# A decoder layer's early products: one of them in four chains, one copy out of the banks, and another order for VectorE

## The chip, the cores and the metric

The kernel runs on one core of a Trainium2 chip. The metric is the device time of one execution in microseconds, of which the profile's span (973.2 us before) is the part between the first and the last instruction. TensorE (PE in the rows) multiplies, ScalarE (ACT) and VectorE (DVE) do elementwise work, GpSimd (POOL) a little of it, SyncE (SP) asks for most transfers.

## The reference

One layer, sequence 1024, width 1024, batch 1, all float32:

```python
h = rms_norm(x, pre_g)
z = jnp.einsum('bsd,de->bse', h, w_in)
qa, ka, va, ga, qb, kb, vb, gb, gk_low = split_columns(z)
...
oa = diff_attention(qa, ka, va, lam)
ob = gla_chunked(qb, kb, vb, log_a)
y = jnp.einsum('bse,ed->bsd', jnp.concatenate([oa, ob], axis=-1), w_out)
return x + rms_norm(y, post_g)
```

The change is in the first 100 us, in the first part of `h @ w_in`: the normalised x times the columns vb of the gated values (1024 of them, 512 at a time here) and the first columns of ka.

## The kernel before

**Products.** `h @ w_in` is done with seven products of half-size blocks in place of eight. h is cut in four blocks of 512 x 512 (h11, h12, h21, h22; kept transposed, 4 tiles of 128 rows each, index j), and a group of weight columns likewise (b11, b12, b21, b22). The products are numbered: 1 is h11 b11, 2 is h12 b21, 5 is s1 (b12 - b11), 6 is s2 (b22 - b12 + b11), 7 is s3 (b22 - b12), 4 is h22 (b21 less the sixth's weights), 3 is s4 b22, with s1 = h21 + h22, s2 = s1 - h11, s3 = h11 - h21, s4 = h12 - s2 (in the code with some signs turned). Results go to PSUM banks named x (1, 6, 7), y (2, 4) and z (5, 3). Groups (0,) and (1,) are the gated values, each with two units of 128 rows of the result, so there are four x banks in all; group 2 is a pair of heads of ka with 128 columns to a block.

**Two parts.** Each operand is split in a rounded high part and the rest (h_hi and h_lo, w for both; the type is fp32r), and each product is hi x hi + lo x hi + hi x lo: three matmuls for each of four tiles, 12 of 128x128 by 128x512 to a chain, 48 for both gated groups. The high part is a cast on ScalarE, the low part a subtraction on VectorE.

**Stages.** `load_x` and `load_gated` ask for x and the weights (xs 0 to 3 are named x, 4 to 7 xt; weights are g_raw, `w_early` is for group 2). `norm_x` scales x, the last four tiles on GpSimd. `first(0)` transposes the first half of x's columns for rows 0 to 511 into four banks with spins between (matmuls on zeros whose result is not used) and `put` makes h11's two parts from each bank: the high one by ScalarE, the low one by VectorE, both reading the bank. `first(1)` does the same for h12 and also copies the banks to f1 on ScalarE. `blocks(j)` transposes a tile of h21 and h22 into two banks, which ScalarE copies to t21 and t22 (named t), and makes a tile of s1; `differences(j)` makes s2, s4 and s3's source. `go(n)` does the next n steps of the table `order`, a step being one product of one group; `prepare` makes the weights up to three steps ahead. The sequence at the end of the function is: `first(0)`, a step, `first(1)`, a step, `blocks(0)`, and so on.

**Order.** The engines run their instructions in the order that the framework's scheduler gives. Matmuls and transposes are kept in program order, and so is what is issued while `pinned` is set; the rest is placed by the scheduler, with `tc.issue_after(a)` placing an instruction behind a. L66 is the helper through which all ScalarE, VectorE and GpSimd work is recorded, L142 the helper for matmuls, L145 for transposes, so tiles and not lines tell the groups apart. Banks are taken from the front of the list `free` and put at its end when their last reader has been issued; weights' parts rotate through five buffers (`ring`).

## Time and profile before

| what | us |
| --- | --- |
| median of three runs (976.01 to 976.57) | 976.54 |
| the profiled execution | 974.95 |
| its span | 973.2 |
| TensorE busy in the span | 956.9 |
| TensorE, first matmul of product 1 | 13.95 |
| TensorE, last of product 4 of the gated groups ends | 100.03 |

The times in the rows count from the start of the span. A timeline row gives start, length, engine, line, operation, output and inputs, shapes and the number of instructions merged in it; in brackets the idle time before it and what ended that. A length is that of the instruction; the next one of the same kind may start a little before its end. In a row of waits stand the waiting instruction, the releaser, the sum, the number and the longest.

### The profile page before, as it was taken

The page shows a single profiled execution, that of the slowest core. Times are in us where ns is not written, and L with a number is a line of the kernel's source. Part 1 is how long each engine was busy: PE and PEld are TensorE (multiplying, and loading weights), DVE is VectorE, ACT ScalarE, POOL GpSimd, SP SyncE. Part 2 cuts the span into 40 slices and gives each one's busy share as a digit, 9 for nine tenths or more (in the row PEclk, how much of TensorE's full clock was granted, in tenths as well). Part 3 has the DMA queues.
Part 4 walks back from the last instruction along what each step waited for, and adds up shares of the span by engine and source line. Part 5 has one row for each costly group of instructions (what it writes and reads, how often), then busy time and mean ns, then how long its engine had stood idle before and what let it go on. Part 6 is the DMA issues. An engine that isn't in the chain of part 4 may idle for free.

```text
span 973.2 us, 14406 instructions
## 1 busy us (share of the span) xinstructions
PE 956.9 (98%) x4641; PEld 797.3 (82%) x4641; DVE 736.5 (76%) x1468; ACT 604.8 (62%) x1166; POOL 190.9 (20%) x262
## 2 busy tenths in 40 slices
PE   8889999999999999999999999999999999999997
PEld 6778788888888888888888888878888888888786
DVE  4797699897687686686766576587888888898555
ACT  8653264764667565576765344366776687887773
POOL 3000002222111211231100002121322222443322
PEclk9999999999999999999999999999999999999999
DMA  9424357578667987996864588997656669994777
GB/s 340 157 69 141 95 158 251 184 251 286 210 211 244 291 264 266 286 289 215 253 185 146 169 243 263 402 296 245 221 176 216 240 193 364 335 288 102 152 205 153
DMA packets 152827, 220.36 MB, mean 226 GB/s; under 512 B 15728, under 2 KB 85360, under 8 KB 152656
## 3 DMA queue, kind: packets, MB, share of 16 engines
q1 hardware_dynamic: 138592, 178.70, 57.3%
q0 software_dynamic: 14160, 40.74, 14.2%
q8 instruction: 37, 0.61, 0.3%
q14 instruction: 38, 0.31, 0.1%
HBM read 133.93 MB, written 88.60 MB: 229 GB/s over the span
## 4 chain that ended last, share of the span: by engine, by line
PE 91%; DMA 4%; DVE 2%; SPq 1%; issue 1%; ACT 1%; DVEq 0%; ACTq 0%
PE x L142 23%; PE y L142 15%; PE z L142 14%; PE ypart L142 12%; PE sc L142 6%; PE po L142 5%; PE yps L142 4%; PE wtr L145 3%; PE gpo L142 3%; DMA ks<-k_d 1%; PE kv L142 1%; DMA g_raw<-in_w_in_dram 1%; DMA q_d<-qk_st 1%; PE gkl_ps L142 1%; PE pa L142 1%
## 5 line engine op out<-in xcount | busy, mean ns | idle before, releaser
L66 ACT CAST w<-w_raw 128x512 fp32r<-128x512 f32 x138 | 85.2, 621 | 80.2 <-PE y L142 34.7
L66 ACT ACTIVATE p<-p,stt 128x896 f32<-128x896 f32 (+7 forms) x128 | 99.3, 776 | 36.8 <-DVE stt L66 35.7
L66 DVE TENSOR_TENSOR w<-w_raw,w 128x512 fp32r<-128x512 f32 x138 | 94.3, 687 | 36.6 <-ACT w L66 36.3
L66 ACT COPY s<-x 128x512 f32<-128x512 f32 x78 | 45.2, 586 | 74.8 <-PE x L142 74.5
L66 DVE CUSTOM_DVE_ANT_0 p<-sc,maskt 128x512 f32<-128x512 f32 (+3 forms) x128 | 74.4, 585 | 15.7 <-PE sc L142 14.5
L66 POOL TENSOR_SCALAR p<-p,stt,lam 128x1024 f32<-128x1024 f32 (+3 forms) x64 | 55.9, 873 | 147.9 <-DVE stt L66 144.0
L142 PE MATMUL z<-s_hi,w 128*128 128x512 f32 x320 | 80.2, 393 | 0.0
L142 PE MATMUL x<-s_hi,w 128*128 128x512 f32 x320 | 80.1, 392 | 0.0
L142 PE MATMUL y<-h_hi,w 128*128 128x512 f32 x320 | 80.1, 392 | 0.0
L142 PE MATMUL ypart<-wo_hi,m_hi 128*128 128x512 f32 x192 | 79.5, 414 | 0.1
L142 PE MATMUL ypart<-wo_hi,m_lo 128*128 128x512 f32 x192 | 75.5, 393 | 0.0
L142 PE MATMUL ypart<-wo_lo,m_hi 128*128 128x512 f32 x192 | 75.4, 393 | 0.0
L66 POOL DMA_DIRECT2D wo_d<-wo_hi x32 | 17.4, 544 | 276.3 <-ACT wo_hi L66 276.3
L142 PE MATMUL sc<-k,q 128*128 128x512 f32 (+1 forms) x192 | 69.0, 363 | 1.3 <-DVE stt L66 1.1
L142 PEld LDWEIGHTS z<-s_hi,w 128*128 128x128 f32 x320 | 59.8, 188 | 12.4
L142 PEld LDWEIGHTS x<-s_hi,w 128*128 128x128 f32 x320 | 59.7, 188 | 12.4
L142 PEld LDWEIGHTS y<-h_hi,w 128*128 128x128 f32 x320 | 59.7, 188 | 12.3
L142 PE MATMUL sc<-ks,q 128*128 128x512 f32 (+1 forms) x192 | 66.1, 348 | 0.3 <-DMA ks<-k_d 0.3
L66 ACT CAST wt_hi<-wtr 128x512 fp32r<-128x512 f32 (+1 forms) x80 | 42.8, 535 | 25.3 <-PE wtr L145 24.5
L66 DVE TENSOR_TENSOR w_raw<-w_raw 128x512 f32<-128x512 f32 x80 | 55.3, 691 | 2.8 <-DMA w_raw<-in_w_in_dram 1.9
L66 DVE TENSOR_TENSOR wt_lo<-wtr,wt_hi 128x512 fp32r<-128x512 f32 (+1 forms) x80 | 50.6, 633 | 8.6 <-ACT wt_hi L66 8.0
L66 DVE TENSOR_TENSOR c<-z,s 128x512 f32<-128x512 f32 x48 | 32.9, 689 | 31.1 <-ACT s L66 19.9
(228 smaller groups left out, 2350.8 us busy)
## 6 DMA issues: line engine op xcount, KB each, us to landing
w_raw<-in_w_in_dram SPq DMA_DIRECT2D x40, 512.0 KB, 4.7
wo_d<-wo_hi POOLq DMA_DIRECT2D x32, 256.0 KB, 3.3
q<-q_d SPq DMA_DIRECT2D x32, 256.0 KB, 4.5
k<-k_d SPq DMA_DIRECT2D x32, 256.0 KB, 5.0
ks<-k_d SPq DMA_DIRECT2D x64, 128.0 KB, 5.7
v<-v_d SPq DMA_DIRECT2D x16, 512.0 KB, 7.0
wo_raw<-in_w_out_dram POOLq DMA_DIRECT2D x31, 256.0 KB, 4.7
wo_d<-gqd POOLq DMA_DIRECT2D x22, 256.0 KB, 4.3
```

The lines of the kernel that those rows point to most:

```text
L66: ins = op(*a, **k)
L142: tc.keep_in_program_order(pe.matmul(*a, **k))
L145: tc.keep_in_program_order(pe.transpose(dst, src, ident))
```

## The change

Three things are changed, all ahead of the third column group.

First, product 1 of the gated values. `gated_first` takes the x banks of all four units at once and runs their chains side by side: sixteen matmuls with both high parts, sixteen with h's low part, sixteen with the weights' low part. Between the second and the third part stand `first(1)`'s transposes. The weights' second half is cast after the first two h_hi. One spin fewer stands before it. On TensorE, around the end of the first transposes, before (spin, then x of the first group's two units, then `first(1)`'s transposes xT):

```order
L142 MATMUL spin<-idle,ones 128x512 x4
L142 MATMUL x<-w,h_hi 128x512 x4
L142 MATMUL x<-w,h_lo 128x512 x4
L142 MATMUL x<-w,h_hi 128x512 x8
L145 MATMUL xT<-ident,x_187 128x128 x8
L145 MATMUL xT<-ident,x_190 128x128 x8
```

and now:

```order
L142 MATMUL spin<-idle,ones 128x512 x3
L142 MATMUL x<-w,h_hi 128x512 x16
L142 MATMUL x<-w,h_lo 128x512 x16
L145 MATMUL xT<-ident,x_187 128x128 x2
L145 MATMUL xT<-ident,x_190 128x128 x2
L145 MATMUL xT<-ident,xt 128x128 x8
```

The four chains have become one run of 16, 16 and 16, with the transposes of x between the second and the third, and those of xt behind. (Rows that only repeat are left out: the other chains before, the other banks' transposes and the last sixteen x<-w,h_hi now.)

Second, `first(1)`: ScalarE copies each bank to f1, and h12's two parts are made from f1, not from the bank. Its transposes go bank by bank. The low halves of product 2's weights lie in the buffers that h22's low part takes later, not in the ring.

Third, VectorE's order. s4 and s2 share a buffer and s4 is made after s3; h22's low part is placed behind the sixth product's weights, s3's behind h22's, and the b22 - b12 + b11 subtractions are issued by themselves. `hold` bounds how far weights are prepared. On VectorE, up to the last of the four subtractions that make s2 (s_684<-t_415,t_414 before, the one s_643<-t_440,t_439 in the second listing; f is f1, t are t21 and t22, s_lo are low parts, c and qk_hi belong to group 2, h_lo is h22's low part, the 128x1024 rows are weights), before:

```order
L66 TENSOR_TENSOR h_lo<-t_415,h_hi 128x512 x4
L66 TENSOR_TENSOR g_raw<-g_raw 128x1024
L66 TENSOR_TENSOR s_657<-f_253,s_659 128x512
L66 SCALAR_TENSOR_TENSOR c<-c,qk_hi 128x512
L66 TENSOR_TENSOR s_657<-f_253,s_670 128x512
L66 TENSOR_TENSOR s_lo<-s_659,s_hi 128x512
L66 TENSOR_TENSOR s_677<-t_415,t_414 128x512
L66 TENSOR_TENSOR s_lo<-s_670,s_hi 128x512
L66 TENSOR_TENSOR w<-g_raw,w 128x1024 x2
L66 TENSOR_TENSOR s_684<-t_415,t_414 128x512
```

and now:

```order
L66 TENSOR_TENSOR g_raw<-g_raw 128x1024 x2
L66 SCALAR_TENSOR_TENSOR c<-c,qk_hi 128x512
L66 TENSOR_TENSOR s_lo<-s_642,s_hi 128x512 x2
L66 TENSOR_TENSOR s_643<-t_440,t_439 128x512
L66 TENSOR_TENSOR s_lo<-s_643,s_hi 128x512 x2
L66 TENSOR_TENSOR w<-g_raw,w 128x1024 x2
L66 TENSOR_TENSOR h_lo<-t_440,h_hi 128x512 x4
L66 TENSOR_TENSOR s_lo<-t_439,s_hi 128x512 x4
```

h_lo, the two s<-f,s and the two w have moved from ahead of the last s2 to behind it.

On ScalarE, at the end of product 7 (g_raw<-x are the copies of the x banks when product 7 is in them, w the casts of product 4's weights, w_raw those of group 2), before:

```order
L66 CAST w_817<-g_raw_813 128x1024
L66 CAST w_818<-g_raw_814 128x1024
L66 COPY g_raw_522<-x_356 128x512
L66 COPY g_raw_522<-x_357 128x512
L66 CAST w_898<-w_raw_889 128x512
L66 COPY g_raw_523<-x_419 128x512
L66 COPY g_raw_523<-x_420 128x512
```

and now:

```order
L66 COPY g_raw_521<-x_355 128x512
L66 COPY g_raw_521<-x_356 128x512
L66 CAST w_812<-g_raw_808 128x1024
L66 COPY g_raw_522<-x_357 128x512
L66 COPY g_raw_522<-x_358 128x512
L66 CAST w_813<-g_raw_809 128x1024
```

The casts stood ahead of the copies; now the second one stands behind all four.

The diff, cut to its core:

```diff
@@ -288,15 +288,16 @@
 
         if i >= len(order) or i in ws:
             return
-        if 2 <= i <= n_early + 1:
+        if i >= hold[0]:
+            return
+        if 2 < i <= n_early + 1:
             with tc.issue_after(act.last), tc.issue_after(dve.last):
-                make_weights(i)
-        elif order[i] in ((0, 6), (0, 7)):
-            with tc.issue_after(behind[0].ins):
                 make_weights(i)
         else:
             make_weights(i)
 
+    hold = [2]
+
     def fetch_raw(p, n, i):
...
 
-        name = {5: "b12", 6: "b22", 4: "b21x"}.get(n)
+        name = {5: "b12", 4: "b21x"}.get(n)
         if name:
             load_gated(name)
...
         src = {1: b11, 2: b21, 5: b11, 6: b11, 7: b12, 4: again, 3: b22}[n]
-        a, b = {5: (b12, b11), 6: (b22, b11), 7: (b22, b12), 4: (again, b11)}.get(n, (None, None))
+        a, b = {5: (b12, b11), 7: (b22, b12), 4: (again, b11)}.get(n, (None, None))
         own = {2: 1, 5: 1, 6: 3, 4: 1}.get(n)
         w = []
         for i in range(4):
             if i == own:
                 w.append(kp.tile([P, 2, 512], F32R, tag="ks1", name="w"))
+            elif n == 2 and i > 1:
+                w.append(hw.tile([P, 2, 512], F32R, tag=f"h22_lo{i - 2}", name="w"))
             else:
                 w.append(ap.tile([P, 2, 512], F32R, tag="ring", name="w", bufs=NRING))
-        for i in range(2):
+        def hi(i):
             if a:
                 dve.tensor_tensor(src[i], a[i], b[i], ALU.subtract)
             act.copy(w[i], src[i])
-        for i in range(2):
-            dve.tensor_tensor(w[2 + i], src[i], fp(w[i]), ALU.subtract)
+
+        def lo(i):
+            lows[n] = dve.tensor_tensor(w[2 + i], src[i], fp(w[i]), ALU.subtract)
+
+        hi(0)
+        if n == 1:
+            lo(0)
+            between.append(lambda: (hi(1), lo(1)))
+        elif n == 7:
+            hi(1)
+            between.append(lambda: (lo(0), lo(1)))
+        else:
+            hi(1)
+            lo(0)
+            lo(1)
         return w[:2], w[2:]
+
+    between, lows = [], {}
...
@@ -510,9 +528,11 @@
...
-        if n in (1, 2, 5, 4):
+        if n in (2, 5, 4) or (n == 1 and p in VALS):
             for b in state:
                 b[name], b["i" + name] = take_bank([P, 512], name)
+        if (p, n) == (0, 1):
+            return gated_first()
         multiply_values(i, [b[name] for b in state], n not in (6, 7, 3))
         gated = p in GATED
         give = take_gated if gated else take_heads
@@ -526,7 +546,8 @@
             if n == 6 or n == (2 if gated else 1):
                 k = "s2" if n == 6 else "s1"
                 b[k] = t2k("s", 4, "s")
-                act.copy(b[k], b["x"])
+                with tc.issue_after(act.last) if k == "s1" else nullcontext():
+                    act.copy(b[k], b["x"])
             if n == 7:
                 b["s3"] = s3[:, u]
                 act.copy(b["s3"], ps)
@@ -536,6 +557,26 @@
                 half, unit, k = {2: (0, 0, "s1"), 4: (1, 0, "s3"), 3: (0, 1, "s2")}[n]
                 give(half * 4 + t, unit, ps, b[k])
                 free.append(b["i" + name])
+
+    def gated_first():
+
+        w = ws.pop(0)
+        ws.pop(1)
+        made[0] = 2
+        units = [b for p in GATED for b in sums.setdefault(p, [{}, {}])]
+        for b in units:
+            b["x"], b["ix"] = take_bank([P, 512], "x")
+        hi, lo = H["h11"]
+        for j, (a, part) in enumerate(((0, hi), (0, lo), (1, hi))):
+            if j == 2:
+                first(1)
+            for k in range(HB):
+                for u, b in enumerate(units):
+                    mm(
+                        b["x"], at(part, k)[:, u * P : u * P + P], w[a][k // 2][:, k % 2, :],
+                        start=(j == 0 and k == 0), stop=(j == 2 and k == HB - 1),
+                        skip_group_check=True,
+                    )
 
     def step(i):
 
@@ -659,23 +700,30 @@
             spin(14)
         for i in range(4):
             for j in range(HB):
-                k = h * HB + j
-                tr(ps[j][0][:, i * P : (i + 1) * P], xs[i][:, k * P : (k + 1) * P])
+                a, b = (j, i) if not h else (i, j)
+                k = h * HB + a
+                tr(ps[a][0][:, b * P : (b + 1) * P], xs[b][:, k * P : (k + 1) * P])
             if not h:
-                spin((3, 7, 3, 4)[i])
+                spin((3, 7, 3, 3)[i])
         hi, lo = H[("h11", "h12")[h]]
-        for j in range(HB):
-            put(ps[j][0], h * HB + j, (hi, lo), j)
-        pinned[0] = not h
+        if h:
+            for j in range(HB):
+                act.activation(f1[:, j], ps[j][0], AF.Copy, scale=pre_g[:, HB + j : HB + j + 1])
         for j in range(HB):
             if h:
-                act.activation(f1[:, j], ps[j][0], AF.Copy, scale=pre_g[:, h * HB + j : h * HB + j + 1])
+                act.copy(at(hi, j), f1[:, j])
+                dve.tensor_tensor(at(lo, j), f1[:, j], fp(at(hi, j)), ALU.subtract)
+            else:
+                put(ps[j][0], j, (hi, lo), j)
+                if j == 1:
+                    between.pop()()
             free.append(ps[j][1])
 
-    def parts(n, j, f):
+    def parts(n, j, f, after=None):
         hi, lo = block(n)
         act.copy(at(hi, j), f)
-        return dve.tensor_tensor(at(lo, j), f, fp(at(hi, j)), ALU.subtract)
+        with tc.issue_after(after.ins) if after else nullcontext():
+            return dve.tensor_tensor(at(lo, j), f, fp(at(hi, j)), ALU.subtract)
 
     def blocks(j):
 
@@ -698,12 +746,12 @@
         return parts("s1", j, s1)
 
     def differences(j):
-        h21, s2 = t21[:, j], t_c("s2")
+        h21, s2 = t21[:, j], s24[j // 2][:, j % 2]
         hi, lo = H["h11"]
         dve.tensor_tensor(h21, fp(at(hi, j)), h21, ALU.subtract)
         dve.tensor_tensor(h21, fp(at(lo, j)), h21, ALU.add)
-        dve.tensor_tensor(s2, t22[:, j], h21, ALU.subtract)
-        dve.tensor_tensor(s4[j // 2][:, j % 2], f1[:, j], s2, ALU.subtract)
+        with tc.issue_after(sums_done.ins):
+            dve.tensor_tensor(s2, t22[:, j], h21, ALU.subtract)
         return parts("s2", j, s2)
 
     made = [0]
@@ -760,33 +808,50 @@
     first(0)
     norm_x(4, 5)
     norm_x(6, 7)
-    go(1)
-    first(1)
+    hold[0] = 4
+    for i in (2, 3):
+        prepare(i)
+    hold[0] = 8
+    step(0)
     t21, t22 = (
         hpool.tile([P, HB, 512], F32, tag=tag, name=name)
         for tag, name in (("s4_hi0", "t21"), ("s3_hi0", "t22"))
     )
-    go(1)
     blocks(0)
     go(1)
     blocks(1)
     go(1)
     blocks(2)
     go(1)
-    behind = [blocks(3)]
-    sums_done = behind[0].ins
+    sums_done = blocks(3)
     go(1)
-    s4 = [kp.tile([P, 2, 512], F32, tag=f"k{i}", name="s4") for i in range(2)]
+    s24 = [kp.tile([P, 2, 512], F32, tag=f"k{i}", name="s24") for i in range(2)]
     for j in range(HB):
-        behind = [differences(j)]
+        ready = differences(j)
+    load_gated("b22")
+    for r, a in zip(gated_raws["b11"], gated_raws["b22"]):
+        with tc.issue_after(sums_done.ins):
+            dve.tensor_tensor(r, a, r, ALU.subtract)
+    hold[0] = 10
+    with tc.issue_after(ready.ins):
+        prepare(8)
+        prepare(9)
+    for j in range(HB):
+        h22_lo = parts("h22", j, t22[:, j], lows[6])
     go(2)
-    with tc.issue_after(sums_done):
-        for j in range(HB):
-            parts("h22", j, t22[:, j])
-        for j in range(HB):
-            behind = [parts("s3", j, t21[:, j])]
-        for j in range(HB):
-            parts("s4", j, s4[j // 2][:, j % 2])
+    for j in range(HB):
+        s3_lo = parts("s3", j, t21[:, j], h22_lo)
+    hold[0] = len(order)
+    with tc.issue_after(s3_lo.ins):
+        prepare(10)
+        prepare(11)
+    for j in range(HB):
+        s = s24[j // 2][:, j % 2]
+        with tc.issue_after(s3_lo.ins):
+            dve.tensor_tensor(s, f1[:, j], s, ALU.subtract)
+    for j in range(HB):
+        behind = [parts("s4", j, s24[j // 2][:, j % 2])]
+    between.pop()()
     go(4)
 
 
```

## The prediction, made before the changed kernel ran

> **What bounds the kernel now.** I read the page's head, TensorE's waits over the first 140 us, and then the timelines of the engines there.
>
> ```profile
> span 973.2 us, 14406 instructions
> 100.00:600.00 500.00, 500.00 (x2374) 418.17 (x2373) 382.33 (x612) 289.11 (x498) 70.64 (x114) 1.00 0.71 227
> PE x L142 <- ACT s_hi L66: 2.7, 1, 2.7
> PE xT L145 <- issue: 2.6, 1, 2.6
> ```
>
> The second row is the stretch from 100 to 600 us (its length, then busy time of TensorE, weight load, VectorE, ScalarE and GpSimd, granted clock, DMA): TensorE is busy for all 500 us. So what is won before 100 us reaches 600 us whole, and nothing but the first 100 us can give much. The last two rows are TensorE's longest waits there. Its timeline (start, length, instructions, idle before them) shows where:
>
> ```profile
> 11.80 0.66 PE L145 MATMUL xT<-ident,x 128*128 128x128 f32 x4
> 12.22 1.17 PE L142 MATMUL spin<-idle,ones 128*128 128x512 f32 x4
> 13.95 2.23 PE L142 MATMUL x<-w,h_hi 128*128 128x512 f32 x4 [0.56 <-ACT h_hi L66]
> 17.61 2.00 PE L142 MATMUL x<-w,h_hi 128*128 128x512 f32 x8
> 21.26 1.91 PE L145 MATMUL xT<-ident,x 128*128 128x128 f32 x16
> 22.92 1.18 PE L142 MATMUL x<-w,h_hi 128*128 128x512 f32 x4
> 27.59 1.07 PE L142 MATMUL x<-w,h_hi 128*128 128x512 f32 x4
> 31.23 1.27 PE L145 MATMUL xT<-ident,xt 128*128 128x128 f32 x8 [2.58 <-issue]
> 32.50 1.20 PE L142 MATMUL y<-w,h_hi 128*128 128x512 f32 x4
> 62.72 1.55 PE L142 MATMUL x<-w,s_hi 128*128 128x512 f32 x6
> 67.00 0.73 PE L142 MATMUL x<-w,s_hi 128*128 128x512 f32 x2 [2.74 <-ACT s_hi L66]
> 74.64 1.98 PE L142 MATMUL x<-w,s_lo 128*128 128x512 f32 x8
> 76.45 3.79 PE L142 MATMUL x<-w,s_hi 128*128 128x512 f32 x16
> 87.33 1.98 PE L142 MATMUL x<-w,s_hi 128*128 128x512 f32 x8
> 89.15 1.98 PE L142 MATMUL y<-w,h_hi 128*128 128x512 f32 x8
> 100.03 2.00 PE L142 MATMUL gkl_ps<-h_hi,wl 128*64 128x512 f32 x8
> 68.00:71.00 3.00, 3.00 (x8) 2.32 (x8) 3.00 (x5) 2.08 (x3) 0.00 (x0) 0.50 0.00 0
> ```
>
> From 76.45 to 87.33 stand 48 matmuls without a wait: 10.88 us, 0.227 each. With that price the losses can be counted. (1) The first eight matmuls take from 13.95 to 17.61, 3.66 instead of 1.81: 1.85 lost inside what counts as busy. (2) The four matmuls at 27.59 are through by 28.50; the next transposes begin at 31.23, and last 1.27 to 32.50: 2.73 lost. (3) Six matmuls from 62.72 are through by 64.08, the seventh starts at 67.00: 2.92 lost. (4) The 26 matmuls from 67.00 to 74.64 take 7.64 instead of 5.89, and the last row says why: for 68 to 71 us the granted clock is 0.50. 1.75 lost. Together 9.25 us of the 86.08 between 13.95 and 100.03.
>
> **The change, part by part.** The rows of the other engines that release these waits:
>
> ```profile
> 12.26 1.05 ACT L66 CAST w<-g_raw 128x1024 fp32r<-128x1024 f32 x1 [0.45 <-DMA g_raw<-in_w_in_dram]
> 13.22 2.41 ACT L66 ACTIVATE h_hi<-xT,pre_g 128x512 fp32r<-128x512 f32 x4
> 20.16 0.18 ACT L66 ACTIVATION_READ_ACCUMULATOR junk<-xt 128x1 f32 x1
> 22.04 1.98 ACT L66 CAST w<-g_raw 128x1024 fp32r<-128x1024 f32 x2
> 30.45 2.00 ACT L66 ACTIVATE f<-xT,pre_g 128x512 f32<-128x512 f32 x3 [1.10 <-DVE h_lo L66]
> 66.33 0.62 ACT L66 CAST s_hi<-s 128x512 fp32r<-128x512 f32 x1 [2.85 <-DVE s L66]
> 89.17 1.08 ACT L66 COPY g_raw<-x 128x512 f32<-128x512 f32 x2
> 17.74 0.23 DVE L1651 TENSOR_SCALAR ssq<-ssq,eps_t 128x2 f32<-128x2 f32 x1 [0.53 <-ACT junk L66]
> 20.38 0.88 DVE L1651 TENSOR_SCALAR ssq<-ssq,eps_t 128x2 f32<-128x2 f32 x1 [1.52 <-ACT junk L66]
> 27.39 2.36 DVE L66 TENSOR_TENSOR w<-g_raw,w 128x1024 fp32r<-128x1024 f32 x2 [4.66 <-PE x L142]
> 29.67 2.72 DVE L66 SCALAR_TENSOR_TENSOR h_lo<-xT,pre_g,h_hi 128x512 fp32r<-128x512 f32 x4
> 34.22 0.69 DVE L66 TENSOR_TENSOR s<-t,t 128x512 f32<-128x512 f32 x1 [1.24 <-ACT t L66]
> 56.19 2.50 DVE L66 TENSOR_TENSOR h_lo<-t,h_hi 128x512 fp32r<-128x512 f32 x4
> 65.61 0.69 DVE L66 TENSOR_TENSOR s<-t,t 128x512 f32<-128x512 f32 x1
> 34.80:66.30 31.50, 29.47 (x142) 24.08 (x140) 30.31 (x44) 15.31 (x23) 2.64 (x3) 1.00 0.29 86
> 19.01 2.22 POOL L66 TENSOR_SCALAR xt<-xt,ssq 128x1024 f32<-128x1024 f32 x2 [6.71 <-DVE ssq L1659]
> 22.88 2.22 POOL L66 TENSOR_SCALAR xt<-xt,ssq 128x1024 f32<-128x1024 f32 x2 [1.65 <-DMA out_dram<-in_x_dram]
> 28.64 1.51 SPq L255 DMA_DIRECT2D g_raw<-in_w_in_dram  x2
> DMA to landing us min/median/max: 5.8/5.9/5.9
> ```
>
> *The start.* Before, both weight casts stand ahead of h_hi, which starts at 13.22. Now two h_hi stand between them. The last transposes begin at 11.80 and need 0.66, the first bank being done near 12.1; h_hi takes 0.6 to the next (2.41 / 4), 0.7 to its end, so TensorE has its operand near 12.85. The spins are three now, not four (1.17 / 4 each), and end near 13.1. Start 13.1 for 13.95: 0.85 won.
>
> *Four chains.* Each h_hi now feeds four matmuls, 0.91 us, and the low parts are first wanted after sixteen, 3.6 us on. The third h_hi stands behind the second cast: 13.3 + 0.95 + 0.7 = 14.95, wanted at 13.1 + 8 x 0.227 = 14.9. So 1.75 of the 1.85 is won.
>
> *One copy out of the banks.* The wait at 31.23 carries no releaser but "issue". The order of banks names it: these transposes take the bank that the second blocks' first transposes left, and that is free when f has been read, at 30.45 + 0.7 = 31.15. The f row waited for h_lo, h_lo (29.67) for the casts' low half (27.39), and that for a weight buffer that TensorE still read (4.66 us idle). Now f is the only reader, four of them right after the transposes, and the low halves of the second product go to buffers that nobody holds. TensorE comes to these transposes at 13.1 + 0.1 + 48 x 0.227 + 1.66 (21.26 to 22.92) = 25.75; ScalarE's sums over xt end at 20.34 (20.16 + 0.18), its two small steps near 20.9, the two casts (1.98) near 22.8, the first two f near 24.1. The bank wait is gone, 2.73 won, and about 0.3 of the 1.27 with it.
>
> *What is late next there.* GpSimd scales the xt tiles that these transposes read. Before, it did so from 22.88 to 25.10 while VectorE had nothing large. Now no copy of x stands between ScalarE's small steps, GpSimd starts near 22.0, and VectorE's two 128x1024 subtractions start there too. The rows at 17.74 and 20.38 are one instruction; the second began inside GpSimd's 19.01 to 21.23, took 0.88 instead of 0.23, and ended at 21.26, with it. If these four take turns, 2.22 + 2 x 1.13 = 4.5 us from 22.0, the xt tiles are whole at 26.5 for 25.75, and h_lo is later by as much. Bounds: nothing (they overlap freely) and 2.3 (both subtractions first and every later step behind them). I take 1.0, nearest to the row.
> The Trainium skill, page "SBUF — State Buffer", section "Who interferes with whom", makes the port pair that VectorE shares with GpSimd an exclusive lock for a whole instruction, and names subtractions with two SBUF inputs against a GpSimd instruction that reads SBUF. This speaks against the change, and the 0.88 agrees; without such a lock the sum below would be 1.0 better.
>
> *VectorE's order.* The wait at 67.00 is for s_hi (66.33), and that for s at 65.61, the fourth of its kind. VectorE is busy for 30.31 of the 31.50 us before it: it is the bound there, and TensorE waits for its queue. In the new order the four h_lo (2.40 to the next, 56.19), two f - s (1.2) and the two low halves of the sixth product's weights (2.3) stand behind the last s: 5.9 us less ahead of it. And the first sum of that queue, s<-t,t at 34.22, starts when ScalarE has both t: f to 25.1, four casts of h_hi at 0.52, two t at 0.57 and 0.7 to the end make 28.4, with the 1.0 above 29.4. So the last s is ready near 66.3 - 5.9 - 4.8 = 55.6. TensorE reaches the sixth product at 64.08 - 1.36 - (0.85 + 1.75 + 2.73 + 0.3 - 1.0) = 58.1 and wants the fourth s_hi at 59.5: some 3 us of cover, after its cast. The weights' low halves then follow near 59, wanted at 58.1 + 3.6. With that both the 2.92 and the 1.75 of half clock are won, 4.67. If the cover is gone, all 4.67 stays lost. Next in line, the seventh product's weights come 2.3 (subtraction) after s_lo of s3 and still ahead of TensorE by about 2 us.
>
> *A wait that is added.* In ScalarE's new order the second cast of the fourth product's weights stands behind the two copies g_raw<-x that wait for TensorE's last matmul of the seventh product; before, both casts stood ahead. The copies start as TensorE moves on (89.17 against 89.15), take 0.98 to the next, the cast 1.05: the weights come 2.07 later. TensorE has four matmuls to do meanwhile, 0.91. It waits 1.2. The clock fell after the idle 2.74 but not after 2.58, so I leave the clock whole; the bound is 1.75 more.
>
> *The loads.* The b12 blocks (28.64; landing after 5.8 and 5.9) are asked for once the low halves are made, now near 24 and 25, and are first read near 33. No cost. From the first product of the third column group on, the order on all engines is as before but for one pair on VectorE, so the gain should pass on unchanged.
>
> **Sum.** 0.85 + 1.75 + 2.73 + 0.3 + 4.67 = 10.3; less 1.0 (GpSimd) and 1.2 (cast) and 0.2 for the h_hi casts that now follow f one by one: 7.9. The profiled execution, 974.95, becomes 967.05; the median of the three runs shown stands 1.59 above it at 976.54 and becomes 968.6.
>
> **Rivals.**
> *The cover is too thin.* VectorE is still the queue that ends last, and s comes late. For it: 30.31 of 31.50 busy. Against it: 5.9 us leave the queue ahead of s and it starts earlier. 4.67 stay lost: 976.54 - 3.2 = 973.3.
> *The clock falls at the new wait.* Two idles of almost one length fell on either side, 2.58 and 2.74; 1.2 is far below both. Then 968.6 + 1.75 = 970.4.
> *No port conflict, no late cast to speak of.* The four GpSimd and VectorE instructions interleave without loss, and the copies start early: up to 2.2 better, 966.4.
> *The gain is eaten later.* From 600 us on TensorE waits for reloads of k and q. They follow TensorE's own products, so they should move too; if they held, all would be spent, 976.5.
> *Slower.* The b12 load now follows the six copies of x to the output at once, at the time of the fullest DMA. The fifth product starts at 62.72 - 10.88 - 4.6 = 47.2 and needs it 2.4 (subtraction and cast) earlier, at 44.8; each us after that is lost, and past 52.7, 28 us after it was asked for, the kernel is slower than before: landing at 55.2 gives 979.0. Against it: 5.9 in the row.
>
> **Chances.** Forecast 0.68 (its own range 967.2 to 970.0), clock 0.10, no conflict 0.10, cover 0.05, eaten 0.04, slower 0.03. The range 966.2 to 971.4 leaves out the last three, and a little of each end. About 0.2%, 2 us, is what a measurement of this kernel can tell from no change; the first four cases are faster by more, 0.93, the fifth is within it, 0.04, the last slower, 0.03.
>
> **What would show it.** Right: the x matmuls start near 13.1 and run without a gap; no idle over 1 us ahead of the first xt transposes; the sixth product without idle and without a 0.50 clock; about 1.2 idle inside the first four matmuls of y after the seventh product, for ScalarE's w; gkl_ps at 92 instead of 100.03. Wrong: a VectorE s still named ahead of TensorE, b12 named by a wait for DMA, or gkl_ps at 92 and a span that is not 8 shorter.

## The result, and the profile after

| | median us | runs | ratio to before, 95% interval |
| --- | --- | --- | --- |
| before, beside it | 976.27 | 4 (975.68 to 976.57) | |
| the changed kernel | 968.0 | 4 (966.8 to 969.13) | 0.9916 [0.9899, 0.9933] |
| the changed kernel, measured once more | 966.55 | 4 (965.9 to 967.31) | 0.9905 [0.989, 0.9919] |

The forecast was 968.6, with a range of 966.2 to 971.4. The two medians of one kernel differ by 1.45 us, so between kernels measured at different times a difference of about 1.5 us says nothing by itself; where it matters the traces decide. The profiled execution is the slowest of its four, 969.13, with a span of 967.4, while the one before, 974.95, lies below its median: the medians are 8.3 us apart, the two profiled executions 5.8.

TensorE's timeline after (start, length, instructions, idle before them), the rows that answer to those of before:

```profile
13.61 4.16 PE L142 MATMUL x<-w,h_hi 128*128 128x512 f32 x16
26.68 1.03 PE L145 MATMUL xT<-ident,xt 128*128 128x128 f32 x8
57.72 1.98 PE L142 MATMUL x<-w,s_hi 128*128 128x512 f32 x8
77.67 1.97 PE L142 MATMUL x<-w,s_hi 128*128 128x512 f32 x8
80.08 1.21 PE L142 MATMUL y<-w,h_hi 128*128 128x512 f32 x4 [0.44 <-ACT w L66]
82.85 1.20 PE L142 MATMUL y<-w,h_hi 128*128 128x512 f32 x4 [1.56 <-ACT w L66]
92.97 2.01 PE L142 MATMUL gkl_ps<-h_hi,wl 128*64 128x512 f32 x8
```

TensorE's waits up to 140 us (sum, number, longest; the first spins' wait of 1.5, which is there before and after, is left out):

```profile
PE y L142 <- ACT w L66: 2.0, 2, 1.6
PE xT L145 <- DVE x L66: 0.5, 2, 0.3
```

And the stretch from 100 to 600 us (busy time of TensorE, weight load, VectorE, ScalarE and GpSimd, clock, DMA):

```profile
100.00:600.00 500.00, 500.00 (x2374) 418.77 (x2372) 378.10 (x607) 289.74 (x499) 83.97 (x123) 1.00 0.72 228
```

Of the four losses that were counted before, three are gone: there is no idle ahead of the xt transposes at 26.68, none in the sixth product at 57.72, and its clock is whole. Of the first, 0.36 of the 1.85 is left: the sixteen matmuls at 13.61 take 3.99 to the next row (17.60), and 16 x 0.227 is 3.63. The 7.06 us won at gkl_ps (92.97 for 100.03) pass through the stretch from 100 to 600, where TensorE is again busy throughout; its first sc matmul behind that stretch starts at 621.1 for 627.9, 6.8 earlier. One wait is new, in product 4. It is longer than its two brackets: the eight matmuls at 77.67 are through at 79.48, the next begins at 80.08, and the four there take until 82.85 and not 0.91. Together 2.46 us, where the prediction had 1.2.

What released it, by the timelines of VectorE, SyncE and ScalarE:

```profile
72.21 2.49 DVE L66 TENSOR_TENSOR s_lo<-s,s_hi 128x512 fp32r<-128x512 f32 x4
73.66 1.66 SPq L255 DMA_DIRECT2D g_raw<-in_w_in_dram  x2
80.50 1.22 DVE L66 TENSOR_TENSOR g_raw<-g_raw 128x1024 f32<-128x1024 f32 x1 [1.55 <-DMA g_raw<-in_w_in_dram]
79.93 1.07 ACT L66 COPY g_raw<-x 128x512 f32<-128x512 f32 x2
81.75 1.04 ACT L66 CAST w<-g_raw 128x1024 fp32r<-128x1024 f32 x1 [0.76 <-DVE g_raw L66]
```

by the DMA issues of that time (number, size, median us to landing):

```profile
g_raw<-in_w_in_dram SPq DMA_DIRECT2D x2, 512.0 KB, 4.8
```

and by the chain of waits (start, length, what):

```profile
74.73 5.67 DMA g_raw<-in_w_in_dram
```

The cast that TensorE waits for starts at 81.75. The two copies ahead of it were done near 81; the subtraction that feeds it ended at 81.72. That subtraction waited for the load of b21x, whose two halves were asked for only as the s_lo of s4 had read the buffers that they go to (72.21 and on; the second half at 74.73, behind the last s_lo). The copies that the prediction blamed are not the last to come. In the second profile of the changed kernel it is the same: the copies were done at 80.15, the subtraction at 80.46, and the cast began at 80.49.

### The profile page after: what moved, and what is told of

It reads as the page before. It is cut to its first block, busy times and chain, and to the rows that moved or that the text cites. A ratio compares the mean times of both kernels' runs of the same rounds, so it can differ in the third digit from the quotient of the medians.

```text
span 967.4 us, 14406 instructions
## 1 busy us (share of the span) xinstructions
PE 953.9 (99%) x4640; PEld 795.3 (82%) x4640; DVE 735.3 (76%) x1468; ACT 603.5 (62%) x1166; POOL 201.6 (21%) x262
## 4 chain that ended last, share of the span: by engine, by line
PE 86%; DMA 5%; DVE 4%; SPq 3%; issue 1%; ACT 1%; DVEq 0%; ACTq 0%
PE x L142 20%; PE z L142 14%; PE y L142 14%; PE ypart L142 12%; PE sc L142 6%; PE po L142 5%; PE yps L142 4%; PE wtr L145 3%; PE gpo L142 3%; DMA g_raw<-in_w_in_dram 3%; DMA ks<-k_d 1%; PE kv L142 1%; DMA k_d<-qk_st 1%; DVE s_lo L66 1%; SPq L472 1%
## 5 line engine op out<-in xcount | busy, mean ns | idle before, releaser
L66 ACT COPY s<-x 128x512 f32<-128x512 f32 x78 | 44.8, 586 | 72.7 <-PE x L142 72.5
```

The source lines that it names most:

```text
L66: ins = op(*a, **k)
```

## The experiments

Theory A is the prediction's: the new wait comes from ScalarE's order. Theory B came out of the trace after: it comes from the load. A second question was whether the three parts add up as the sum has them.

**The cast ahead of the copies (e_cast).**

```diff
-            act.copy(w[i], src[i])
+            casts[n] = act.copy(w[i], src[i])
...
-                act.copy(b["s3"], ps)
+                with tc.issue_after(casts[4].ins) if p == GATED[1] else nullcontext():
+                    act.copy(b["s3"], ps)
```

> The changed kernel with one thing moved on ScalarE: the last two of the four copies g_raw<-x at the end of product 7 stand behind the second cast of product 4's weights, not ahead of it. Theory A (the prediction's: ScalarE's order makes TensorE wait in product 4): the cast comes 1 us earlier, the two waits there (0.44 and 1.56 in the changed kernel) shrink by 1 to 1.2 together, and the median falls from 968.0 to about 966.9. Theory B (the load of the weights b21x decides: it is asked for at 73.66, when the last s_lo of s4 has read the buffer, and VectorE's subtractions at 77.72 and 80.50 wait for it): the cast still starts only when the subtraction that began at 80.50 is done, near 81.75, TensorE waits as long as before, and the median stays within 0.4 us of 968.0.

Median 968.02 (966.87 to 969.35), ratio 0.9919 [0.9902, 0.9937]: nothing won. VectorE's, ScalarE's and TensorE's timeline of it:

```profile
78.79 1.23 DVE L66 TENSOR_TENSOR g_raw<-g_raw 128x1024 f32<-128x1024 f32 x1 [0.79 <-DMA g_raw<-in_w_in_dram]
80.05 1.05 ACT L66 CAST w<-g_raw 128x1024 fp32r<-128x1024 f32 x1 [0.96 <-DVE g_raw L66]
81.15 1.20 PE L142 MATMUL y<-w,h_hi 128*128 128x512 f32 x4 [0.82 <-ACT w L66]
```

With no copy ahead of it the cast still starts when the subtraction ends (80.02), and TensorE still waits for it. The wait in product 4 is shorter here, 1.14 for the 2.46 and 1.62 of the changed kernel, which is what theory A asked for in size; but it is the subtraction that came earlier (78.79 for 80.50), since its load was asked for 0.7 earlier and landed after 4.2 and not 4.8, in the fastest of the four runs. So the order is not what TensorE waited for, and theory A falls for the changed kernel.

**The load asked for earlier (e_load).** s4 goes to four buffers of its own.

```diff
+    s4s = []
     for j in range(HB):
         s = s24[j // 2][:, j % 2]
         with tc.issue_after(s3_lo.ins):
-            dve.tensor_tensor(s, f1[:, j], s, ALU.subtract)
+            s4s.append((t_c if j < 2 else t_st)("s4"))
+            dve.tensor_tensor(s4s[j], f1[:, j], s, ALU.subtract)
     for j in range(HB):
-        behind = [parts("s4", j, s24[j // 2][:, j % 2])]
+        behind = [parts("s4", j, s4s[j])]
```

> The changed kernel with s4 written to four small buffers of its own and not over s2, so that the buffer that b21x is loaded to is free once the four s4 are computed (near 69.5) and not after their low parts (near 73.6). The scheduler then places the second cast of product 4's weights ahead of the last two copies g_raw<-x by itself, as when only that is done. Theory B (the load decides): b21x is asked for about 4 us earlier, its two subtractions on VectorE follow near 75 and 77, both casts are done before TensorE reaches product 4, both waits there go, and the median falls by their sum less some tenths, 2.2 to 2.5, to about 965.7. Theory A (ScalarE's order decides): the same as with the cast moved alone, 966.9; the earlier load adds nothing.

Median 964.76 (964.49 to 965.31), ratio 0.9886 [0.9871, 0.9901]. All four runs lie below all eight of the changed kernel (965.9 the lowest) and below the four of e_cast, which were measured beside them (966.87 the lowest). The median is 3.2 below the changed kernel's first and 1.8 below its second, where 965.7, 2.2 to 2.5 below the first, was expected; the intervals of the ratio just meet for the second (0.9901 and 0.989), so the traces have to decide. SyncE's, VectorE's and TensorE's timeline of it:

```profile
68.22 1.47 SPq L255 DMA_DIRECT2D g_raw<-in_w_in_dram  x2
73.25 1.22 DVE L66 TENSOR_TENSOR g_raw<-g_raw 128x1024 f32<-128x1024 f32 x1
75.12 1.22 DVE L66 TENSOR_TENSOR g_raw<-g_raw 128x1024 f32<-128x1024 f32 x1
79.27 1.98 PE L142 MATMUL y<-w,h_hi 128*128 128x512 f32 x8
90.15 2.01 PE L142 MATMUL gkl_ps<-h_hi,wl 128*64 128x512 f32 x8
```

and the engines' busy time from 13.6 to 100 us, in the columns as above:

```profile
13.60:100.00 86.40, 86.40 (x404) 69.70 (x404) 76.07 (x114) 50.46 (x83) 10.85 (x11) 1.00 0.56 172
```

The load is asked for 5.4 earlier, neither subtraction waits for it, product 4 runs without a break, and TensorE is busy for all of the 86.40 us. Theory B holds. With the load early, the framework's scheduler also put both casts ahead of the last two copies (the second cast at 76.37, the copies at 79.30); whether the copies would hold the cast up if they stood ahead of it then was not run. They come close: in u_copy below, where the subtraction ended at 80.06, the cast began at 80.36 behind a copy. Nothing is left to win in that stretch but what lies inside the busy time.

**The changed kernel once more (after_again).**

> The changed kernel once more, beside the others of this call. Its times of before spread over 2.3 us (966.8 to 969.13), those of the kernel with the earlier load only over 0.8. If the wait for b21x in product 4 is what spreads them, a second profile shows another length of that wait with another landing time (between about 1 and 2.5 for landings of 3.8 to 4.8), and TensorE's other waits ahead of 100 us unchanged; its median is 968.0 within 0.8.

Median 966.55. TensorE's timeline:

```profile
79.06 1.09 PE L142 MATMUL y<-w,h_hi 128*128 128x512 f32 x4
81.59 1.19 PE L142 MATMUL y<-w,h_hi 128*128 128x512 f32 x4 [1.44 <-ACT w L66]
91.71 2.00 PE L142 MATMUL gkl_ps<-h_hi,wl 128*64 128x512 f32 x8
```

and the load of b21x among the DMA issues:

```profile
g_raw<-in_w_in_dram SPq DMA_DIRECT2D x2, 512.0 KB, 4.6
```

Product 4 began at 79.06 here, so the wait is 81.59 - 79.06 - 0.91 = 1.62, for 2.46 in the first profile; between the first x matmul and product 4 TensorE has no other wait in either. The wait does differ from run to run, and it is 0.84 of the 1.26 between the two at gkl_ps (0.35 is a later start, 13.61 for 13.26). The landing medians, 4.6 and 4.8, are too close to carry that alone: the load was also asked for 1 us earlier. The median lies 0.65 below what was expected, 968.0 within 0.8.

**One part undone (u_order, u_four, u_copy, u_part2).** Each is the changed kernel without one part; the core of each edit, in that order:

```diff
-        h21, s2 = t21[:, j], s24[j // 2][:, j % 2]
+        h21, s2 = t21[:, j], t_c("s2")
...
+        dve.tensor_tensor(s4[j // 2][:, j % 2], f1[:, j], s2, ALU.subtract)
...
-        if (p, n) == (0, 1):
-            return gated_first()
...
-        if h:
-            for j in range(HB):
-                act.activation(f1[:, j], ps[j][0], AF.Copy, scale=pre_g[:, HB + j : HB + j + 1])
+        for j in range(HB):
+            put(ps[j][0], h * HB + j, (hi, lo), j)
...
-            elif n == 2 and i > 1:
-                w.append(hw.tile([P, 2, 512], F32R, tag=f"h22_lo{i - 2}", name="w"))
```

(u_part2 is the last two together, u_copy the third alone. One piece of the second part stays in all four: the transposes of `first(1)` go bank by bank.)

> The changed kernel without its third part: VectorE's order is again that of the kernel before (s4 beside s2, h22's low parts, two f - s and the sixth product's low halves ahead of the last s2), the four chains and the one copy out of the banks stay. Additive theory (each part is worth its term of the sum): TensorE reaches the sixth product at 57.7, VectorE's queue begins 4.8 earlier than before and so the last s2 comes at 65.6 - 4.8 = 60.8 and its cast lets TensorE on at 62.2; idle of about 3 as before, the granted clock falls to 0.50 for some 3.4 us, 4.7 lost again; the wait in product 4 (2.46) goes, as TensorE is later: 968.0 + 4.7 - 2.5 = 970.2. Rival (VectorE's queue alone sets the sixth product, and it does not begin earlier, since the load of b12 now lands after 10.8 and not 5.9): the last s2 stays near 65, TensorE waits 6 to 7 there, and the median goes back to 974 to 976.

Median 970.5 (968.73 to 971.87), ratio 0.9941 [0.9919, 0.9963]; 970.2 was expected. TensorE's timeline:

```profile
62.70 1.22 PE L142 MATMUL x<-w,s_hi 128*128 128x512 f32 x2 [2.74 <-ACT s_hi L66]
97.00 2.01 PE L142 MATMUL gkl_ps<-h_hi,wl 128*64 128x512 f32 x8
```

and the engines' busy time around it, the granted clock third from the end:

```profile
62.50:68.50 6.00, 5.80 (x14) 4.56 (x15) 6.00 (x10) 4.32 (x7) 0.00 (x0) 0.50 0.07 11
```

The wait for the last s2 and the half clock are back, and the wait in product 4 is gone, since TensorE comes there at 86.1, long after the load. The half clock lasts twice as long as before (6 us and more); more of this below.

> The changed kernel without its first part: product 1 again in two-unit chains, group after group, both weight casts ahead of the first h_hi, the fourth spin back, the second blocks' transposes after the first group's product. Additive theory: 0.85 + 1.75 are lost, TensorE is 2.6 later everywhere and VectorE's queue with it, so the wait in product 4 stays and the median is 970.6. Rival (the wait in product 4 is at a time that VectorE and the load of b21x set, and TensorE's lead there is only idle time): the lost 2.6 are taken out of that wait, which falls from 2.46 to near 0, and the median stays at 968.0 to 968.5.

Median 968.96, ratio 0.9925 [0.9909, 0.9941]: between the two expectations, nearer to the rival. In its profile TensorE is at the first y matmuls 2.33 later than in the first profile of the changed kernel (29.79 for 27.46), but only 0.67 later at gkl_ps (93.64 for 92.97): the wait in product 4 has shrunk from 2.46 to 1.09 and taken up most of the rest. Against the second profile of the changed kernel it is 1.93 later. What the chains win at the start is in part waited away again at product 4.

> The changed kernel without the copy of its second part: h12's two parts are again made from the banks, ScalarE's h_hi and VectorE's h_lo first, the copies f behind them. The low halves of product 2's weights stay in the buffers that nobody holds. Theory P (one reader per bank is what freed them, the prediction's 2.73 + 0.3): TensorE waits 2.5 to 3 ahead of the first xt transposes again, and the median rises to about 970 (3.0, of which the wait in product 4 takes up about half, as it did when the four chains were undone). Rival Q (the weight buffer that TensorE still read held VectorE 4.66 us before h_lo, and that alone kept the banks): h_lo can start near 25 at once, the first bank is read by 26.5, TensorE's wait there stays under 1, and the median is within 0.8 of 968.0.

Median 967.89, ratio 0.9916 [0.9902, 0.9931]: no loss. The first xt transposes begin at 26.42, without a wait; 0.66 is lost in product 7 for its weights, and product 4 waits 0.71. Theory P falls and rival Q fits: with a free weight buffer, h12's parts may read the banks and TensorE does not notice.

> The changed kernel without its whole second part: h12's parts are made from the banks, and the low halves of product 2's weights come from the ring again; the four chains and VectorE's order stay. Additive theory (the second part is worth its term, 2.73 + 0.3, beside the four chains as without them): TensorE waits 2.5 to 3 ahead of the first xt transposes again, about half of it is taken out of the wait in product 4, and the median is 969.5. Rival (the four chains read product 1's high weights for the last time near 21, not 28.5, and so free the same ring buffers before VectorE wants them at 22.4): no idle of VectorE over 1 us there, TensorE's wait stays under 1, and the median is within 0.8 of 967.5 (between the two medians of the changed kernel, 968.0 and 966.6).

Median 966.4, ratio 0.9893 [0.9875, 0.991]: no loss either, and 0.3 below the rival's range. VectorE's and TensorE's timeline:

```profile
22.05 2.36 DVE L66 TENSOR_TENSOR w<-g_raw,w 128x1024 fp32r<-128x1024 f32 x2
26.30 1.03 PE L145 MATMUL xT<-ident,xt 128*128 128x128 f32 x8
```

VectorE's low halves start at 22.05 without idle before them, out of the ring: the four chains read product 1's high weights for the last time near 21, so the ring has room by then. Beside the four chains the copy and the buffers are worth nothing. The order of the transposes, which stayed, does not decide it here: they are all done by 22.54, and ScalarE, the first to read the banks, comes to them at 22.87, behind its casts.

**One part alone (a_buf, a_four, a_copy, a_order).** All four put the low halves of product 2's weights in the new buffers. a_buf is the kernel before with nothing else:

```diff
+            elif n == 2 and i > 1:
+                w.append(hw.tile([P, 2, 512], F32R, tag=f"h22_lo{i - 2}", name="w"))
```

The other three keep one part more of the change: `gated_first` with its spin and its cast order; f1 first in `first(1)`; VectorE's order at the end of the function. They were made from the changed kernel by undoing the other two parts, and are not quite the kernel before with one part, as their expectations have it: in all three the weights of product 2 are also prepared ahead of the first step, the transposes of `first(1)` go bank by bank, and `pinned` is no longer lifted there. Only a_buf differs from the kernel before in one thing.

> The kernel before with one edit: the low halves of product 2's weights lie in the two buffers that h22's low part takes later, not in the ring. Product order, bank reading and VectorE's order stay. Theory Q (the ring buffer that TensorE still read was what kept the banks): VectorE's 4.66 us of idle ahead of these w rows go, h_lo starts near 24.5 and not 29.67, TensorE's wait of 2.58 ahead of the first xt transposes is gone (they begin near 28.7), VectorE's queue begins some 3 earlier, the idle for the last s2 and the 0.50 clock stay: 2.0 to 2.9 won, 973.2 to 974.1. Theory P (the banks need one reader each): the wait stays above 1.5 and the median within 0.8 of 976.0.

Median 971.38 (970.98 to 973.07), ratio 0.9949 [0.9934, 0.9964]: two lines won 5.3 in the median (3.5 to 6.4 by the interval), more than the 2.0 to 2.9 of theory Q, which holds in its mechanism. Timelines of VectorE and TensorE:

```profile
23.65 3.10 DVE L66 TENSOR_TENSOR w<-g_raw,w 128x1024 fp32r<-128x1024 f32 x2 [0.39 <-ACT w L66]
29.04 1.03 PE L145 MATMUL xT<-ident,xt 128*128 128x128 f32 x8
64.29 0.73 PE L142 MATMUL x<-w,s_hi 128*128 128x512 f32 x2 [2.74 <-ACT s_hi L66]
95.69 2.01 PE L142 MATMUL gkl_ps<-h_hi,wl 128*64 128x512 f32 x8
```

and the stretch in which u_order had the clock at 0.50:

```profile
62.50:68.50 6.00, 4.21 (x19) 3.49 (x20) 6.00 (x9) 3.91 (x7) 1.06 (x2) 1.00 0.09 16
```

The idle of 4.66 ahead of the w rows is down to 0.39, and the wait ahead of the xt transposes is gone. The wait for s2 is 2.74 as before, but here no half clock follows it, which theory Q had not expected: that is 1.6 of the 4.34 won at gkl_ps, the buffers are the rest, 2.7.

> The kernel before with the first part alone (four chains, one spin fewer, the second cast behind two h_hi); the low halves of product 2's weights lie in the new buffers here too, the rest is as before. Additive theory: 2.4 to 2.6 won at the start and passed on, since VectorE's queue begins as much earlier: 973.5; if the new buffers alone also free the banks, up to 2.7 more, 970.8. Rival (what TensorE wins at the start it waits longer for the last s2, as VectorE's queue is full): the idle in the sixth product grows from 2.74 to about 5, and the median stays within 0.7 of 976.0.

Median 969.65 (967.63 to 970.48), ratio 0.9931 [0.9911, 0.995]. TensorE is 5.20 earlier at the first y matmuls (27.30 for 32.50), waits 2.74 for s2 at 62.10, and the half clock follows: 4.91 of the 5.20 are left at gkl_ps (95.12). VectorE's queue moved with TensorE, as the additive theory has it with the buffers included; the median moved by 1.6 more than that. Most of this is the choice of the profiled execution of before: the two profiled executions, 974.95 and 969.58, are 5.4 apart.

> The kernel before with the second part alone (one copy out of the banks, h12's parts from f1, new buffers for the low halves). Additive theory: 2.73 + 0.3 less 0.1 won ahead of the first xt transposes, VectorE's queue begins as much earlier, the idle for the last s2 stays near 2.7 with the 0.50 clock behind it: 973.1. Rival (VectorE's queue does not begin earlier): the idle there grows to about 5.5, and the median stays within 0.7 of 976.0.

Median 974.7 (973.29 to 975.97, 10 runs), ratio 0.9983 [0.9974, 0.9993]. TensorE and VectorE:

```profile
66.20 1.22 PE L142 MATMUL x<-w,s_hi 128*128 128x512 f32 x2 [4.83 <-ACT s_hi L66]
50.63 1.23 DVE L66 TENSOR_TENSOR g_raw<-g_raw 128x1024 f32<-128x1024 f32 x1 [1.21 <-DMA g_raw<-in_w_in_dram]
98.98 2.01 PE L142 MATMUL gkl_ps<-h_hi,wl 128*64 128x512 f32 x8
```

Here the rival has the better part: TensorE is 2.62 earlier at the first y matmuls (29.88), but VectorE's queue only 0.8 at the last s2 (64.81 for 65.61), as it waits for a load of weights on the way and has another order; so the idle grows by 2.09 and eats most of it; 1.05 is left at gkl_ps. The same buffers without the copy (a_buf) gave 4.34 there, 1.6 of it by the clock; the rest of the difference can be the copy or the other order that a_copy has, and no run parts the two.

> The kernel before with the third part alone (VectorE's order, with one buffer for s2 and s4; the product order and the bank reading of before; the new buffers for product 2's low halves stay). Additive theory: the idle for the last s2 and the slow clock behind it go (4.7 won), the b21x load now follows s4's low parts and costs 1 to 2.5 in product 4: 972.5 to 973.8. Rival (TensorE, later by about 5 here than in the changed kernel, gives the load the time it needs): no wait in product 4, 971.3.

Median 968.99 (967.9 to 969.62), ratio 0.9927 [0.9912, 0.9941]: 7.2 won, better than both expectations, which had left the buffers out. TensorE is at the first y matmuls 3.07 earlier than before (29.43), does not wait for s2, keeps its clock, and loses 0.71 in product 4 (the second four matmuls at 82.78, the first at 81.16); gkl_ps comes at 92.90, 7.1 earlier: 3.07, and the 2.92 and 1.75 of idle and half clock, less the 0.71.

**The port of VectorE and GpSimd (e_port).** The kernel of e_load with product 2's low halves behind the h_lo of h12:

```diff
+        elif n == 2:
+            hi(1)
+            late.append(lambda: (lo(0), lo(1)))
...
+        if h:
+            with tc.issue_after(last.ins):
+                late.pop()()
```

> The kernel of e_load with one thing moved on VectorE: product 2's two 128x1024 low halves (w) stand behind the four h_lo of h12 and not ahead of them, so that nothing large runs on VectorE while GpSimd scales the last two xt tiles. If the two engines hold each other up there (GpSimd 4.19 for the two tiles beside VectorE's 2.36): GpSimd takes 2.2 again and the tiles are whole near 24.8, not 26.8. Theory M (TensorE comes to them at 26.5 in any case, so the conflict costs 0.1 to 0.3): the time is that of e_load, 964.8, less at most 0.3; h_lo and the sums behind the low halves come later by up to 2.3, inside the cover of the sixth product. Theory N (the prediction's 1.0 for the conflict): 963.8. If GpSimd still takes over 4 us, its slowness is not VectorE's doing.

Median 967.66 (966.98 to 968.05), ratio 0.9914 [0.9898, 0.9931]: 2.9 above e_load, measured at another time, where both theories had it the same or better; at gkl_ps it is 1.8 behind (below). GpSimd's timeline in the changed kernel:

```profile
22.59 4.19 POOL L66 TENSOR_SCALAR xt<-xt,ssq 128x1024 f32<-128x1024 f32 x2 [0.84 <-ACT w L66]
```

in this one:

```profile
22.27 2.23 POOL L66 TENSOR_SCALAR xt<-xt,ssq 128x1024 f32<-128x1024 f32 x2 [0.83 <-ACT w L66]
```

and TensorE's here:

```profile
26.31 1.03 PE L145 MATMUL xT<-ident,xt 128*128 128x128 f32 x8
30.66 1.66 PE L142 MATMUL y<-w,h_hi 128*128 128x512 f32 x6 [0.40 <-DVE w L66]
38.31 1.19 PE L142 MATMUL y<-w,h_hi 128*128 128x512 f32 x4 [0.57 <-DVE gv_st L66]
```

GpSimd takes 2.23 again, so VectorE's two subtractions were what held it up. TensorE begins the xt transposes at 26.31, no earlier than with the conflict (26.30 in the second profile of the changed kernel): the conflict costs it nothing, as theory M has it. The loss is another: w and the order behind it come too late for product 2, and 1.8 are lost at gkl_ps (91.92 for 90.15). The expectation had not asked who needs w.

## Why the prediction was right, and where not

*What bounds the kernel, and the sum.* Right: what was won ahead of 100 us, 7.06, was still 6.8 at 621 us. The sum had gkl_ps at 92.1; the two profiles have 92.97 and 91.71. That it came out so close is in part luck. In the first profile TensorE came to the xt transposes 0.9 later than the sum has it (26.68 for 25.75), the 1.0 for GpSimd was not lost, and the wait in product 4 cost 1.26 more than its term: three errors of about 1 us, one of them with the other sign. And the forecast of 968.6 added 1.59 from the profiled execution to the median, as before; after, the profiled execution lies 1.13 above its median.

*The start, and four chains.* Nearly right. The x matmuls start at 13.61 and 13.26 for 13.1, so 0.3 and 0.7 of the 0.85 were won. They run 16, 16 and 16 without an idle; from 13.26 to the xt transposes at 26.30 are 13.04, for 12.65 predicted.

*One copy out of the banks.* The size was right, the wait of 2.58 is gone. The chain that the step read (f behind h_lo, h_lo behind the low halves, these behind a weight buffer that TensorE read) was right to its last link, and that link is the cause. The step then put the gain down to both the single reader and the new buffers, and to this part alone. The runs say: the buffers alone do it (a_buf), the copy adds nothing beside them and the chains (u_copy), and beside the four chains neither is needed (u_part2). So the terms of the sum were not independent: the chains' gain and the bank's are both had by the first part.

*What is late next there.* The mechanism was right and the size wrong: 1.0 predicted, nothing to be seen. GpSimd did take 4.19 for 2.22, and e_port shows VectorE to be the reason; but TensorE came at 26.7 and 26.3, not 25.75, when the tiles were about ready (26.78 in the first profile). The Trainium skill, page "SBUF — State Buffer", section "Who interferes with whom", calls this an exclusive lock; the 4.19 against 2.23 agrees.

*VectorE's order.* Right: the last s2 is ready at 56.05 (55.36 + 0.69; 55.6 predicted), TensorE is at the sixth product at 57.72 (58.1) and neither waits nor slows. Undoing it (u_order) brought back both the idle and the half clock. The rival "The cover is too thin" is out.

*A wait that is added.* This is the step that failed: it named the wrong releaser, and the wait was 2.46 and 1.62, where 1.2 was predicted. That a wait came at the predicted place all the same is luck. The prediction looked at the copies between the casts on ScalarE and not at what else the new order moves: s2 and s4 lie in the buffers that b21x is loaded to, so s4's low parts, now later, hold the load back. e_cast and e_load settle it. The rival "The clock falls at the new wait" did not come; the clock stayed whole at 1.00 through 1.56 of idle.

*The loads.* "No cost" was right, the landing was not: b12 took 10.8 and not 5.9; it was asked for 5 us earlier, while the copies of x to the output were under way. VectorE's first subtraction on it starts at 34.41, after 1.67 of waiting for it, and the cover of some 10 us held; the rival "Slower" needed it later than 44.8.

*The gain is eaten later.* No, though not every tenth arrives: between gkl_ps and the end the first profile loses 1.3 of its 7.06 (967.4 for 973.2 in span, 5.8). TensorE's waits from 100 us on are 0.8 longer in it (2.9 for 2.1, most of it ahead of sc and ypart); the rest is open. That stretch varies: in the 14 profiles it takes from 872.0 to 874.6 us, so spans that differ by less say little of the first 100 us.

## What to carry to other kernels

When a chain of waits ends in a buffer that is still being read, try the buffer alone first: two lines that gave product 2's low halves a place of their own won 4.34 us at gkl_ps (1.6 of it by the clock), and in the changed kernel the copy that was made for the same wait added nothing to them. When instructions are moved later, list what their inputs' buffers are reused for: a load that waits for the last reader moves with them, and a buffer more (e_load) can be worth more than another order of the waiting engine. Parts of a change that free the same resource do not add up; only undoing each beside the others, and doing each alone, shows which one is needed.

## What was not expected of the hardware

The granted clock does not follow the length of an idle. Four kernels (before, u_order, a_four, a_buf) have the same idle of 2.74 us in the sixth product. By the windows of half a microsecond, the clock is 0.50 afterwards for 3.4 us in the kernel before (from 67.9), for 3.4 in a_four (from 63.3), for 6.8 in u_order (from 62.1, while TensorE was still idle), and not at all in a_buf. The 26 matmuls behind it take 7.64, 7.64, 8.92 and 6.01 us: one and the same wait costs between 0.1 and 3.0 on top of itself. In a_copy 4.83 us of idle were followed by 3.4 too (from 65.8). The rows of a_four (its timeline, then the busy times with the clock third from the end),

```profile
62.10 0.73 PE L142 MATMUL x<-w,s_hi 128*128 128x512 f32 x2 [2.74 <-ACT s_hi L66]
63.50:66.50 3.00, 3.00 (x9) 2.32 (x8) 3.00 (x4) 1.67 (x3) 0.00 (x0) 0.50 0.00 0
```

and of a_copy, in the columns of the second:

```profile
66.00:69.00 3.00, 2.80 (x7) 2.22 (x8) 3.00 (x4) 3.00 (x6) 0.00 (x0) 0.50 0.00 0
```

So the prediction's reading, that 2.58 and 2.74 lie on either side of a limit, was wrong. Times of 3.4 and twice that, at changing distances from the idle, look like a clock that is set anew every 3.4 us by how busy TensorE was in that time; this was read from five traces and not tested by a run of its own. The two idles of the kernel before fit it, by an estimate from these figures: counted back from 67.9 in steps of 3.41, one such boundary falls near 30.3, inside the 2.58 from 28.65 on, and leaves about 1.65 and 0.93 on its two sides, while the 3.41 us that end at 67.9 hold 2.55 of the 2.74. How much idle it takes is open: the 3.41 us ahead of each fall hold 2.1 us of it or more. In u_order TensorE was still idle for the first 0.6 us of the half clock, and a second such stretch followed; in a_copy it was idle for the first 0.5, and none followed. The Trainium skill, page "TensorE: Matmul & The Clock Gate", section "What's actually happening", has such a free-running window of 3413 ns, and the durations agree; its advice against idle over about 3 us, in the section "Why this matters for your kernels", would have let 2.74 pass, and in three of the four kernels with that idle the clock fell.

A load asked for earlier came hardly earlier. b12 was asked for at 23.79 in the changed kernel, while the six copies of x to the output were under way, and landed after 10.8; in e_port it was asked for at 29.55 and landed after 4.6. VectorE's first subtraction on it started at 34.41 and 34.09. The two kernels between them fit (a_buf, asked for at 25.64, landed after 8.7; before, at 28.64, after 5.9): in all four the load was there near 34.5.
